# Reordering ScalarE's work around the values of a sparse-attention branch, and copying two pairs of queries on GpSimd

## The chip, the cores and the metric

The kernel runs on one core of a Trainium2 chip. The metric is device time in microseconds (us) for one execution of the whole program, from its inputs in device memory to its output there. A measurement of this kernel is the median of several executions; beside it stands one profiled execution with its trace.

## The reference, cut to what matters

The reference is one layer of a streaming encoder on x of 512 x 1024. A projection feeds two attention branches of 8 heads of 64 each, gates merge the branches, and a gated MLP with a short causal convolution follows. In outline:

```python
proj = x @ w_in
q_a, k_a, v_a, q_i, k_i, w_i, q_s, k_s, v_s, g_a, g_b = split(proj)
# branch A: an indexer scores all keys, 128 of them are kept per query
sel    = top_k(sum_h w_i * relu(q_i . k_i / 8), 128)
p      = softmax(q_a . k_a[sel] / 8 + bias)       # 8 heads
y_a    = p @ v_a[sel]
# branch B: stick-breaking attention, 8 heads
y_s    = stick_break(q_s . k_s / 8) @ v_s
merged = sigmoid(g_a) * (y_a @ w_dsa) + sigmoid(g_b) * (y_s @ w_sb)
x = layer_norm(alpha * x + merged @ w_out)
u, g = split(x @ w_ffn_in)
x = layer_norm(alpha * x + (gelu(conv(u)) * g) @ w_ffn_out)
```

## The kernel before

**Precision.** Every matrix product is done as three matmuls: each operand is split into a high part (type fp32r) and a low part (what is left), and high x high, high x low and low x high are summed in PSUM. So every weight piece of 128 x 1024 that comes from memory is first split. `Stream` does that: its `load` issues the transfer into one of three `raw` buffers (L71), and `_advance` writes the high part with a ScalarE copy (L101, `whi`) and the low part with a subtraction (L107, `wlo`) on VectorE, or on GpSimd for the keys in `POOL_LO`. High and low parts live in rings of three buffers each, so a split needs the buffer of the piece three places before it, and has to wait until TensorE is done with that piece. `st.asp` says by how many pieces the splits run ahead of the piece that is being fetched: 3.

**Order of the work.** `FILL` (L33) lists the projections in the order in which they are used up: ... `qa1 ka1 va bs0 bs1 qa2 ka2 bs2 bs3 qa3 ka3 ga0` .... Here qaN and kaN are the queries and keys of heads 2N and 2N+1 of branch A ("pair N"), va are the values of branch A for all heads, bsN are the gated products of branch B. These pieces are fed as fillers between the steps of the heads. The heads are walked in one list of sixteen: head 0 to 7 are branch B, head 8 to 15 are branch A, so "head 10" is the third head of branch A (`h` = 2 in the code).

**One head of branch A** goes through these steps:

- TensorE makes the logits (`l_ps`, L538), four blocks of queries in three PSUM banks.
- GpSimd has added the bias window and the selection (`bm`, L527) beforehand. VectorE adds `bm` to the logits and takes the minimum (L544), ScalarE takes the exponential (L546). `ups[h]` keeps the exponential traced last.
- `divide` (L549): VectorE divides by the sums (L550, L553). `send_planes` then cuts the result into two 16-bit halves, one copied by ScalarE (L443), one by VectorE (L444), and the sync queue issues two transposing transfers (L446, `pl<-bm`).
- `join_planes` joins the two transposed halves again into `back`, one by ScalarE (L453) and one by VectorE (L454), and then splits the result into high (`pth`, ScalarE, L456) and low (`ptl`, VectorE, L457).
- `weigh` multiplies these with the values (`av_ps`, L471).

In the loop at L660, the turn of head h makes the logits of head h+1, then weighs head h-1, then divides head h+1, then joins head h.

**The values of branch A.** `proj_v("va", ...)` keeps four PSUM banks open, one per block of 128 rows; these are all the banks of the pool `psA`. It takes four weight pieces, va0 to va3. In the last piece the steps are sorted by block, so that the blocks finish one after the other. Then for every block ScalarE copies it out (L261) and VectorE subtracts (L262), which frees the bank. The first matmul that needs a bank of `psA` afterwards belongs to bs0 (L564).

**Doubling the queries.** `stack_dup` puts the 64 rows of one head's queries, high and low part, into one half of a tile of 128 partitions and copies them into the other half: 64 partitions by 1024 elements. That copy is a transfer issued on ScalarE's queue (L337), two for each pair. Its rows are named qa3a, qa3b and so on.

**What sets the order.** The program is traced in Python order. A planner then simulates a timeline and lays down a fixed order for every engine and queue: what its timeline has as ready goes, and what was traced earlier goes first. On the chip each engine runs its list in that order. `tc.issue_after(ins)` adds one rule to it: what is traced inside the block on the engine of `ins` stands behind `ins` on that engine. It says nothing to other engines. At L679 and L681 it is used like this: the division of head 10 stands behind the last value subtraction (VectorE), and VectorE's half of a joining stands behind the division traced just before it.

Of the kernel before, what the change touches and what calls it, by code (L numbers as in the profile page):

```python
# [14 lines left out]
AF = mybir.ActivationFunctionType  # L15
# [33 lines left out]
def r32(ap):  # L49
    return ap.bitcast(F32)  # L50
# [71 lines left out]
def tile_block(ctx: ExitStack, tc: tile.TileContext, xT, xN, w_qi, w_ki, w_t, w_v, w_br, w_o, w_fi, w_fo,  # L122
               bg, cw, rel, onehot, lnp, out):
    nc = tc.nc
# [72 lines left out]
    st = Stream(tc, rawp, ring, order, 3, 3, place, POOL_LO, DMA_LO)  # L197
# [35 lines left out]
    emptied = {}  # L233

    def proj_v(which, name):

        pss = [(pb if which == "vs" else pa)(f"{name}_ps{i}") for i in range(NB)]
        for g in range(4):
            halves = which == "vs" and g == 0
            if not halves:  # L240
                wh, wl = st.get(f"{which}{g}")
            steps = [(kk, i) for kk in range(2) for i in range(NB)]
            if which == "va" and g == 3:
                steps.sort(key=lambda t: t[1])
            for kk, i in steps:
                k = 2 * g + kk
                c = slice(kk * 512, kk * 512 + 512)
                if halves:
                    if i == 0:
                        wh, wl = st.get(f"{which}{g}{kk}")  # L250
                    c = slice(0, 512)
                r = slice(i * 128, i * 128 + 128)
                nc.tensor.matmul(pss[i], xh[k][:, r], wh[:, c], start=(k == 0), stop=False)
                nc.tensor.matmul(pss[i], xh[k][:, r], wl[:, c], start=False, stop=False)
                nc.tensor.matmul(pss[i], xl[k][:, r], wh[:, c], start=False, stop=(k == KC - 1))
                yield 3
        vt = []
        for i in range(NB):
            v = bp.tile([128, H, 2, 64], F32R, tag="v", bufs=4, name=f"{name}{i}")
            src = pss[i].rearrange("p (h d) -> p h d", h=H)  # L260
            nc.scalar.activation(v[:, :, 0, :], src, AF.Copy)  # L261
            emptied[which] = nc.vector.tensor_sub(v[:, :, 1, :], src, r32(v[:, :, 0, :])).ins  # L262
            vt.append(v)
        return vt

# [3 lines left out]
    xh, xl = [], []  # L269
    qps = [pa(f"qi_ps{n}") for n in range(4)]  # L270
    values = proj_v("vs", "vs")
    ohf = bp.tile([64, NREL], F32, tag="beta", bufs=2, name="ohf")
    rbf = padded(bp, [32, H], name="rbf")
# [12 lines left out]
    for k in range(KC):  # L286
        load_x(k + 3)
        xr = xrs.pop(k)
        h = xp.tile([128, 512], F32R, tag="xh", bufs=KC, name=f"xh{k}")
# [40 lines left out]
    def stack_dup(ps, scale, name):  # L330

        a = bp.tile([128, 2, 512], F32R, tag="q", bufs=4, name=f"{name}a")
        b = bp.tile([128, 2, 512], F32R, tag="q", bufs=4, name=f"{name}b")
        for t, own, oth in ((a, slice(0, 64), slice(64, 128)), (b, slice(64, 128), slice(0, 64))):
            nc.scalar.activation(t[own, 0], ps[own], AF.Copy, scale=scale)
            nc.vector.scalar_tensor_tensor(t[own, 1], ps[own], scale, r32(t[own, 0]), op0=ALU.mult, op1=ALU.subtract)
            nc.scalar.dma_start(r32(t[oth]), r32(t[own]))  # L337
        return a, b


# [63 lines left out]
    def select_some(n):  # L404
        for _ in zip(range(n), rounds):
            pass


    def turned():
        return (bp.tile([128, ATT], F32R, tag="th", bufs=1, name="pth"),  # L410
                bp.tile([128, ATT], F32R, tag="tl", bufs=1, name="ptl"))

    def turn_weights(a, off=OFF):

        groups = ((0, ((0, 0),)), (512, ((1, 0), (3, 384))), (1024, ((2, 0),)))
        th, tl = turned()
        parts = []
        for base, grp in groups:
            ps = pb("tr_ps")
            width = 0  # L420
            for i, o in grp:
                for j in range(i, NB):
                    c = off[j] + i * 128
                    nc.tensor.transpose(ps[:, o + (j - i) * 128:o + (j - i) * 128 + 128], a[:, c:c + 128], ident)
                width = max(width, o + 512 - 128 * i)
            w = slice(base, base + width)
            nc.scalar.activation(th[:, w], ps[:, :width], AF.Copy)
            lows = nc.vector.tensor_sub(tl[:, w], ps[:, :width], r32(th[:, w]))
            for i, o in grp:
                c = slice(base + o, base + o + 512 - 128 * i)  # L430
                parts.append((i, slice(128 * i, 512), th[:, c], tl[:, c]))
        parts.sort(key=lambda t: t[0])
        return parts, lows.ins

    def halves16(t):
        return t.bitcast(U16).rearrange("p (c two) -> p two c", two=2)
# [12 lines left out]
    def join_planes(pl):  # L449

        back = bp.tile([128, ATT], F32, tag="back", bufs=1, name="back")
        got = pl.rearrange("p a b c -> p a (b c)")
        nc.scalar.activation(halves16(back)[:, 1], got[:, 1], AF.Copy)  # L453
        nc.vector.tensor_copy(halves16(back)[:, 0], got[:, 0])  # L454
        th, tl = turned()
        nc.scalar.activation(th, back, AF.Copy)  # L456
        nc.vector.tensor_sub(tl, back, r32(th))  # L457
        h, l = (t.rearrange("p (s c) -> p s c", c=128) for t in (th, tl))
        parts = [(i, o, h[:, c], l[:, c]) for i, o, c in
                 ((0, slice(128, 512), slice(0, 9, 3)), (0, slice(0, 128), slice(2, 3)),  # L460
                  (1, slice(128, 512), slice(1, 9, 3)), (2, slice(256, 512), slice(5, 9, 3)),
                  (3, slice(384, 512), slice(9, 10)))]
        return parts
# [42 lines left out]
    def sb_sticks(beta, keep):  # L506

        for j in (0, 2, 3, 1):
            N = 128 * (j + 1)
            lo, hi = OFF[j], OFF[j] + N  # L510
            rev = keep[:, hi:lo:-1]
            scan = nc.vector.tensor_tensor_scan(rev, rev, first[:, 512 - N:512][:, ::-1], 0.0, op0=ALU.mult,  # L512
                                                op1=ALU.max)
        nc.gpsimd.tensor_mul(beta, beta, keep[:, 1:ATT + 1])  # L514
        return scan.ins


    ups = {}
# [83 lines left out]
    def fill(n):  # L602
        while n > 0:
            c = next(fillers, None)
            if c is None:
                return
            n -= c
# [31 lines left out]
    def start_head(i):  # L639
        w, h = heads[i]  # L640
        fill_until(f"q{w}{h//2}", f"k{w}{h//2}")
        if i == H:
            select_some(99)
        args = qk[f"q{w}{h//2}"][h % 2], qk[f"k{w}{h//2}"][h % 2], h
        return sb_head(*args) if w == "s" else dsa_head(*args)

    weights = start_head(0)
    sb_sticks(*weights)
    fill_until("qs1", "ks1")
    def values_of(parts, w, h):  # L650
        if h % 2 == 0:
            pair[w] = bp.tile([128, 512], F32, tag="yt", bufs=2, name=f"y{w}t{h//2}")
        fill_until(f"v{w}")
        ends = weigh(parts, vals[w], h, pair[w])
        if h % 2 == 1:
            (ys if w == "s" else ya).append(finish_pair(pair[w], f"y{w}{h//2}"))
        return ends

    pair, joined = {}, None
    for i, (w, h) in enumerate(heads):  # L660
        following = start_head(i + 1) if i + 1 < len(heads) else ()
        fill(GAP)
        if w == "s":
            parts, lows = turn_weights(weights[0])
            if len(following) == 2:
                with tc.issue_after(lows):
                    scan = sb_sticks(*following)
                with tc.issue_after(scan):
                    select_some(ROUNDS[i])
            fill(GAP)  # L670
            values_of(parts, w, h)
            if len(following) == 1:
                following = following[0]()
        else:
            if joined is not None:
                values_of(*joined)
            fill(GAP)
            if following:
                with tc.issue_after(emptied["va"]) if h == 1 else nullcontext():  # L679
                    following = following[0]()  # L680
                with tc.issue_after(following[1]):  # L681
                    parts = join_planes(weights[0])
            else:
                parts, _ = turn_weights(weights[0], SOFF)
            joined = parts, w, h
        fill(GAP)
        weights = following
# [275 lines left out]
    def bank_c(name):  # L963
        return psC.tile([128, 512], F32, tag="C", bufs=2, name=name)
# [5 lines left out]
    for f in range(2, FC):  # L970
        ups = bank_c("u_ps")
# [240 lines left out]
```

## Time and profile before

| | |
|---|---|
| median of 3 runs | 759.39 us (757.17 to 759.42) |
| the profiled execution | 759.3 us, of which its span is 757.5 us |
| mean granted TensorE clock | 0.996 |
| TensorE (PE) busy | 743.1 us, 98% of the span |
| VectorE (DVE) busy | 564.6 us, 75% |
| ScalarE (ACT) busy | 397.2 us, 52% |
| GpSimd (POOL) busy | 134.2 us, 18% |
| branch A's heads on the timeline | about 188 to 328 us |
| last value matmul of branch A | starts at 225.56 us |

Times of the trace are counted from the start of the span; the 1.8 us by which the execution is longer than its span lie outside of it. The page gives busy times; what sets the end is read from the waits and from the chain that ended last. In a timeline row the columns are the start and the duration in us, the engine, the line of the kernel, the operation, its tiles (written <- read), and in brackets how long the engine stood idle before it and what released it. PEld is TensorE's loading of weights. A name with a small q (SPq, ACTq) is an engine's queue, which issues transfers.

### The profile page before, as it was taken

To read this page: it belongs to the slowest core of one execution; us is meant where nothing else is said; L and a number is where in the kernel's file an instruction comes from. 1 tells how busy PE (TensorE), PEld (TensorE's weight loads), DVE (VectorE), ACT (ScalarE), POOL (GpSimd) and SP (SyncE) were. 2 spreads that over 40 slices of the span, in tenths; PEclk is the share of its full clock that TensorE was granted. 3 is DMA by queue.
4 is the path that set the end of the run, shared out by engine and by line. 5 is a ranking of instruction groups with operands and counts; after the bars stand their busy time and mean duration, and the time that the engine had idled before them with its cause. 6 is when DMAs were issued, how large, how long until landed. Compare 5 with 4: busy or idle time off the path is not lost.

```text
span 757.5 us, 9792 instructions
## 1 busy us (share of the span) xinstructions
PE 743.1 (98%) x3517; PEld 622.3 (82%) x3517; DVE 564.6 (75%) x906; ACT 397.2 (52%) x572; POOL 134.2 (18%) x158
## 2 busy tenths in 40 slices
PE   9999999999999999999999999999999999999996
PEld 7877888888877887888889888888888888888885
DVE  5569777799878795758864867766776767668985
ACT  5475867665575576946364634433443344346430
POOL 0001324223652222000011110011011101110011
PEclk9999999999999999999999999999999999999999
DMA  7445877672374547426823444434444443448542
GB/s 267 149 131 194 206 167 171 137 180 71 98 180 133 146 129 135 119 62 216 333 56 84 139 150 143 158 134 153 139 139 144 148 140 131 147 135 283 195 138 83
DMA packets 60831, 114.80 MB, mean 152 GB/s; under 512 B 29480, under 2 KB 29736, under 8 KB 60784
## 3 DMA queue, kind: packets, MB, share of 16 engines
q1 hardware_dynamic: 53184, 90.70, 38.4%
q0 software_dynamic: 5744, 18.38, 9.7%
q10 hardware_dynamic: 1856, 5.11, 3.0%
q8 instruction: 27, 0.44, 0.3%
q14 instruction: 20, 0.16, 0.1%
HBM read 95.93 MB, written 9.98 MB: 140 GB/s over the span
## 4 chain that ended last, share of the span: by engine, by line
PE 96%; DVE 2%; DMA 1%; ACT 1%; issue 1%; SPq 0%; DVEq 0%; ACTq 0%
PE u_ps L852 5%; PE u_ps L851 5%; PE g_ps L852 5%; PE u_ps L850 5%; PE g_ps L851 5%; PE g_ps L850 5%; PE av_ps L471 3%; PE m L931 2%; PE m L932 2%; PE m L930 2%; PE gb_ps L228 2%; PE ga_ps L229 2%; PE ga_ps L227 2%; PE gb_ps L227 2%; PE gb_ps L229 2%; PE ga_ps L228 2%
## 5 line engine op out<-in xcount | busy, mean ns | idle before, releaser
L101 ACT ACTIVATE whi<-raw 128x1024 fp32r<-128x1024 f32 (+1 forms) x124 | 124.1, 1001 | 172.8 <-PE g_ps L851 45.3
L107 DVE TENSOR_TENSOR wlo<-raw,whi 128x1024 fp32r<-128x1024 f32 (+1 forms) x105 | 123.2, 1174 | 46.7 <-ACT whi L101 46.1
L852 PE MATMUL u_ps<-x1h,wlo 128*128 128x512 f32 (+1 forms) x192 | 71.4, 372 | 0.0
L850 PE MATMUL u_ps<-x1h,whi 128*128 128x512 f32 (+1 forms) x192 | 71.3, 372 | 0.0
L851 PE MATMUL u_ps<-x1l,whi 128*128 128x512 f32 (+1 forms) x192 | 71.3, 371 | 0.0
L850 PE MATMUL g_ps<-x1h,whi 128*128 128x512 f32 (+1 forms) x184 | 69.9, 380 | 0.0
L851 PE MATMUL g_ps<-x1l,whi 128*128 128x512 f32 (+1 forms) x184 | 69.9, 380 | 0.0
L852 PE MATMUL g_ps<-x1h,wlo 128*128 128x512 f32 (+1 forms) x184 | 69.9, 380 | 0.0
L851 PEld LDWEIGHTS u_ps<-x1l,whi 128*128 128x128 f32 x192 | 36.2, 188 | 6.3
L850 PEld LDWEIGHTS u_ps<-x1h,whi 128*128 128x128 f32 x192 | 36.2, 188 | 6.3
L852 PEld LDWEIGHTS u_ps<-x1h,wlo 128*128 128x128 f32 x192 | 36.2, 188 | 6.2
L851 PEld LDWEIGHTS g_ps<-x1l,whi 128*128 128x128 f32 x184 | 34.6, 188 | 6.6
L850 PEld LDWEIGHTS g_ps<-x1h,whi 128*128 128x128 f32 x184 | 34.6, 188 | 6.5
L852 PEld LDWEIGHTS g_ps<-x1h,wlo 128*128 128x128 f32 x184 | 34.6, 188 | 6.5
L527 POOL TENSOR_TENSOR bm<-win,score 128x256 f32<-128x256 f32 (+2 forms) x24 | 29.7, 1265 | 50.4 <-DMA pl<-bm 29.9
L873 DVE TENSOR_TENSOR t<-raw 128x512 f32<-128x512 f32 x11 | 7.6, 692 | 37.8 <-DMA raw<-in_w_fo_dram 37.8
L906 DVE TENSOR_TENSOR hF<-g_ps,c 128x512 f32<-128x512 f32 x22 | 15.1, 687 | 20.8 <-PE g_ps L852 20.8
L898 ACT ACTIVATE c<-c,cwt 128x512 f32<-128x512 f32 x22 | 15.9, 724 | 25.4 <-DVE c L897 25.2
L892 POOL MEMSET u<- 128x2 f32 x22 | 2.1, 99 | 147.1 <-ACT whi L101 101.1
L397 DVE MAX8 m<-score 128x8 f32<-128x256 f32 (+2 forms) x48 | 26.5, 554 | 0.9
L514 POOL TENSOR_TENSOR beta<-beta,keep 128x1280 f32<-128x1280 f32 x8 | 19.6, 2453 | 37.2 <-DVE keep L512 28.3
L748 POOL TENSOR_TENSOR rstd<-rstd,mhalf 128x1 f32<-128x1 f32 x8 | 7.7, 959 | 104.0 <-DVE rstd L747 104.0
(571 smaller groups left out, 2062.4 us busy)
## 6 DMA issues: line engine op xcount, KB each, us to landing
raw<-in_w_fi_dram SPq DMA_DIRECT2D x44, 512.0 KB, 3.3
raw<-in_w_t_dram SPq DMA_DIRECT2D x32, 512.0 KB, 3.4
raw<-in_w_fo_dram SPq DMA_DIRECT2D x26, 512.0 KB, 3.9
wlo<-in_w_t_dram POOLq DMA_DIRECT2D x14, 512.0 KB, 5.5
raw<-in_w_br_dram SPq DMA_DIRECT2D x8, 512.0 KB, 3.3
raw<-in_w_o_dram SPq DMA_DIRECT2D x8, 512.0 KB, 4.0
raw<-in_w_v_dram SPq DMA_DIRECT2D x7, 512.0 KB, 3.3
raw_b<-in_w_fo_dram SPq DMA_DIRECT2D x6, 512.0 KB, 5.5
```

The costliest lines, as they stand in the source:

```text
L101: nc.scalar.activation(hi[:, :w], t[:, :w], AF.Copy)
L107: self.done[key] = eng.tensor_sub(lo[:, :w], t[:, :w], r32(hi[:, :w])).ins
L227: nc.tensor.matmul(ps[:M], wh[:, c], xh[k], start=(k == 0), stop=False)
L228: nc.tensor.matmul(ps[:M], wh[:, c], xl[k], start=False, stop=False)
L229: nc.tensor.matmul(ps[:M], wl[:, c], xh[k], start=False, stop=(k == KC - 1))
L397: nc.vector.max(m8, sc)
L471: nc.tensor.matmul(dst, vt[i][:, h].rearrange("p a d -> p (a d)"), t, start=(n == 0), stop=(n == len(seq) - 1))
L514: nc.gpsimd.tensor_mul(beta, beta, keep[:, 1:ATT + 1])
L527: nc.gpsimd.tensor_add(bm[:, SOFF[j]:SOFF[j] + N], win[:, 512 - N:512], score[j])
L850: nc.tensor.matmul(ps[:, c], wh[:, kc], x1h[:, k, c], start=(k == 0), stop=False)
L851: nc.tensor.matmul(ps[:, c], wh[:, kc], x1l[:, k, c], start=False, stop=False)
L852: nc.tensor.matmul(ps[:, c], wl[:, kc], x1h[:, k, c], start=False, stop=(k == KC - 1))
```

## The change

There are three edits.

1. In `proj_v`, while the piece va3 is fetched, `st.asp` is 2 in place of 3, and 3 again afterwards. The split of qa2, which was traced while va3 was fetched, is now traced with the next fetch (bs0), behind the values' copies and subtractions.
2. `emptied` keeps both the ScalarE copy and the VectorE subtraction of the last value block. What is traced for the division of head 10, and the joining of head 9 that follows it, stands behind both, each on its own engine. Every joining also stands, on ScalarE, behind the last exponential of the next head (`ups[h + 1]`).
3. For qa2 and qa3 the doubling is a GpSimd `tensor_copy` of 64 x 1024 in place of a transfer on ScalarE's queue. The other pairs keep the transfer.

```diff
@@ proj_v
             if not halves:
+                st.asp = 2 if (which, g) == ("va", 3) else 3
                 wh, wl = st.get(f"{which}{g}")
+                st.asp = 3
@@ proj_v, the end
-            nc.scalar.activation(v[:, :, 0, :], src, AF.Copy)
-            emptied[which] = nc.vector.tensor_sub(v[:, :, 1, :], src, r32(v[:, :, 0, :])).ins
+            copied = nc.scalar.activation(v[:, :, 0, :], src, AF.Copy)
+            emptied[which] = copied.ins, nc.vector.tensor_sub(v[:, :, 1, :], src, r32(v[:, :, 0, :])).ins
@@ stack_dup
-            nc.scalar.dma_start(r32(t[oth]), r32(t[own]))
+            if name in ("qa2", "qa3"):
+                nc.gpsimd.tensor_copy(t[oth], r32(t[own]))
+            else:
+                nc.scalar.dma_start(r32(t[oth]), r32(t[own]))
@@ the loop over heads
             if following:
-                with tc.issue_after(emptied["va"]) if h == 1 else nullcontext():
+                behind = emptied["va"] if h == 1 else ()
+                with ExitStack() as ties:
+                    for ins in behind:
+                        ties.enter_context(tc.issue_after(ins))
                     following = following[0]()
-                with tc.issue_after(following[1]):
-                    parts = join_planes(weights[0])
+                    with tc.issue_after(following[1]), tc.issue_after(ups[h + 1]):
+                        parts = join_planes(weights[0])
```

## The prediction

> **What bounds the kernel now.** I read the page first: the busy times, then the chain of work that ended last.
>
> ```profile
> PE 743.1 (98%) x3517; PEld 622.3 (82%) x3517; DVE 564.6 (75%) x906; ACT 397.2 (52%) x572; POOL 134.2 (18%) x158
> ...
> PE 96%; DVE 2%; DMA 1%; ACT 1%; issue 1%; SPq 0%; DVEq 0%; ACTq 0%
> ```
>
> TensorE (PE) is the bound: 98% busy and 96% of the chain. The change takes no matmul away, so it can only win the time in which PE stands or runs slowly. The next view is what PE waits for, over the whole span.
>
> ```profile
> PE bs_ps L564 <- DVE va L262: 3.0, 1, 3.0
> PE l_ps L538 <- issue: 1.5, 1, 1.5
> ```
>
> Two waits lie in branch A, where all three edits lie: 3.0 us at the first product behind the values, and 1.5 us at a head's logits. What else PE waits for comes before branch A. Third, the busy time by stretches (PE, weight loads, DVE, ACT, POOL, then the granted clock, DMA share, GB/s):
>
> ```profile
> 225.00:229.00 4.00, 0.98 (x5) 0.52 (x4) 2.34 (x3) 4.00 (x7) 2.15 (x3) 1.00 0.37 131
> 229.00:233.00 4.00, 4.00 (x13) 3.32 (x13) 3.96 (x10) 0.51 (x2) 0.00 (x0) 0.57 0.65 205
> 299.50:335.00 35.50, 35.50 (x175) 30.14 (x174) 21.85 (x41) 25.32 (x43) 0.00 (x0) 1.00 0.37 107
> ```
>
> For the 4 us behind the first wait the granted clock is 0.57. So that wait costs more than its 3.0 us: 4 x (1 - 0.57) = 1.7 us are lost to the slow clock, and these count as busy. Behind the second, shorter wait the clock stays at 1.00.
>
> **The first wait, place A.** The timeline of ACT, then of DVE and PE, around the end of the values' matmuls (228.81 - 3.02 = 225.8 us, by the PE row):
>
> ```profile
> 223.01 0.73 ACT L546 ACTIVATE lg<-lg,mn 128x512 f32<-128x512 f32 x1 [0.69 <-DVE mn L544]
> 223.64 0.19 ACT L546 ACTIVATION_READ_ACCUMULATOR lg<-lg,mn 128x1 f32 x1
> 224.06 1.68 ACT L453 ACTIVATE back<-pl 128x1280 uint16<-128x1280 uint16 x1 [0.23 <-DMA pl<-bm]
> 225.58 1.05 ACT L101 ACTIVATE whi<-raw 128x1024 fp32r<-128x1024 f32 x1
> 226.51 1.56 ACT L261 ACTIVATE va<-va_ps 128x512 fp32r<-128x512 f32 x3
> 227.95 1.07 ACT L101 ACTIVATE whi<-raw 128x1024 fp32r<-128x1024 f32 x1
> 228.89 0.61 ACT L261 ACTIVATE va<-va_ps 128x512 fp32r<-128x512 f32 x1
> ```
>
> ```profile
> 222.89 1.22 DVE L107 TENSOR_TENSOR wlo<-raw,whi 128x1024 fp32r<-128x1024 f32 x1
> 226.66 1.50 DVE L107 TENSOR_TENSOR wlo<-raw,whi 128x1024 fp32r<-128x1024 f32 x1 [2.55 <-ACT whi L101]
> 228.07 1.87 DVE L262 TENSOR_TENSOR va<-va_ps,va 128x512 fp32r<-128x512 f32 x3
> ```
>
> ```profile
> 228.81 0.50 PE L564 MATMUL bs_ps<-ys0h,whi 128*128 128x512 f32 x1 [3.02 <-DVE va L262]
> ```
>
> PE needs the bank of value block 0, which is free when the first subtraction on line 262 ends (228.07 + 1.87/3 = 228.7). On DVE that subtraction stands behind a weight split (226.66), which waits for its high part on ACT (225.58), which stands behind the joining of head 9 (224.06). Counting the splits back from the four of va on GpSimd, the one at 225.58 is bs1's and the one at 227.95 is qa2's. So the joining is on the path that sets the end, though nobody needs its result yet.
>
> **The second wait, place B.** DVE, ACT, the two queues and PE:
>
> ```profile
> 296.96 1.40 DVE L107 TENSOR_TENSOR wlo<-raw,whi 128x1024 fp32r<-128x1024 f32 x1 [6.18 <-ACT whi L101]
> 298.38 0.69 DVE L544 CUSTOM_DVE_ANT_0 lg<-l_ps,bm 128x512 f32<-128x512 f32 x1
> ```
>
> ```profile
> 282.92 0.47 ACTq L337 DMA_DIRECT2D qa3a<-qa3a  x1
> ...
> 284.79 0.47 ACTq L337 DMA_DIRECT2D qa3b<-qa3b  x1
> ...
> 294.35 1.67 ACT L453 ACTIVATE back<-pl 128x1280 uint16<-128x1280 uint16 x1 [5.71 <-DMA pl<-bm]
> 295.89 1.04 ACT L101 ACTIVATE whi<-raw 128x1024 fp32r<-128x1024 f32 x1
> ```
>
> ```profile
> 272.30 2.91 SPq L446 DMA_TRANSPOSE pl<-bm  x2
> ...
> 282.75 7.36 SPq L446 DMA_TRANSPOSE pl<-bm  x2
> ```
>
> ```profile
> DMA to landing us min/median/max: 3.4/3.5/11.5
> ```
>
> ```profile
> 299.18 0.70 PE L538 MATMUL l_ps<-ka3b,qa3b 128*128 128x512 f32 x2 [1.47 <-issue]
> ```
>
> The transposes of head 13 go out at 282.75, in the same 2 us as the two doublings of pair 3. Their issue takes 7.36 us where the pair before took 2.91, and the slowest transpose lands after 11.5 us where the median is 3.5. ACT waits 5.71 us for it at the joining; the split behind it comes late; DVE stands 6.18 us at that split's low part; behind it stands line 544, which empties the bank of head 14's logits (298.38 + 0.69 = 299.07). PE starts head 15's logits at 299.18. The page names no releaser, but that bank fits to 0.1 us.
>
> **The change part by part.**
>
> *The joining behind the values' copies (place A).* With the joining gone from its place, ACT is free when the exponential's second part ends, at 223.64 + 0.19 = 223.8. Bs1's high part starts there and not at 225.58, and the low part, the first subtraction and PE all move up by the same 1.8 us. PE restarts at about 227.0, after a gap of 1.2 us in place of 3.0. Bounds: 0, if the planner puts something else as long there; 3.0, if it puts block 0's copy and subtraction ahead of bs1's split, since three quarters of the last piece's matmuls come behind block 0's. I take 1.8: bs1's split is traced earlier than the copies.
>
> *The slow clock behind it.* A gap of 1.47 us left the clock at 1.00, a gap of 3.02 brought 0.57. A gap of 1.2 lies on the side of the former: 1.7 us won. Bounds 0 and 1.7. [...]
>
> *The split of qa2 behind the copies.* It takes 1.07 us of ACT from between the third and fourth value copy, and a low part of 1.2 us (the row at 222.89) from DVE. That brings block 3 and head 10's division forward; PE has other products by then, so 0. If qa2's own split comes later, the cover is the products of bs0 and bs1, which come before qa2's; without it the 1.07 + 1.2 = 2.3 us of the split would be seen there.
>
> *Joinings behind the next head's exponentials.* Same instructions, later on ACT. The farthest move is head 11's, from ahead of head 12's logits to behind its exponentials. There the profile has
>
> ```profile
> 270.05 1.06 ACT L101 ACTIVATE whi<-raw 128x1024 fp32r<-128x1024 f32 x1 [1.77 <-PE bs_ps L565]
> ```
>
> ```profile
> 270.14 0.91 DVE L454 COPY back<-pl 128x1280 uint16<-128x1280 uint16 x1
> ```
>
> an ACT that stands 1.77 us where the joining needs 1.68, ahead of VectorE's half at 270.14, which sets the end of the joining already. So 0. At place B the joining no longer holds up ACT while its transpose is under way: this alone removes the wait there.
>
> *GpSimd's copies for pairs 2 and 3.* Removed: four transfers, 4 x 0.47 us of ACT's queue. Added: four copies of 64 x 1024 on GpSimd. The nearest rows:
>
> ```profile
> L619 POOL CAST oh<-ohf x1: 714/714/714, 19.0 to 19.0; 64x640 fp32r<-64x640 f32 x1
> ```
>
> ```profile
> L107 POOL TENSOR_TENSOR wlo<-raw,whi 128x1024 fp32r<-128x1024 f32 x5 | 12.5, 2499 | 2.7 <-ACT whi L101 2.7
> ```
>
> From below 0.71 x 1024/640 = 1.1 us, from above 2.5 us, which has two inputs; I take 1.3, nearer to the row of its own kind. GpSimd is 18% busy. The copies end some 2 to 4 us after their inputs, the transfer of qa3b took 9.3 us to land. With them gone the transposes have the DMA engines to themselves: at place B a second cure of the same wait. Won there, by either: 1.5 us, bounds 0 and 1.5.
>
> The sum: 1.8 + 1.7 + 1.5 = 5.0 us. The profiled execution took 759.3 us, 0.1 below the median of the runs, and 759.3 - 5.0 = 754.3.
>
> **The rivals.**
>
> *Half of it.* The gap at A stays long enough for the slow clock, or B stays. For it speaks that nothing here shows the clock between gaps of 1.47 and 3.02, and that the planner's order isn't seen. 759.3 - 1.8 - 1.5 = 756.0, or 759.3 - 1.8 - 1.7 = 755.8.
>
> *The wait moves to the next pair's queries.* PE is 3.5 us earlier behind A, but if VectorE isn't, the logits of heads 12 and 14 wait for their queries and keys:
>
> ```profile
> 260.74 0.69 DVE L327 TENSOR_TENSOR ka2b<-ka_ps,ka2b 64x512 fp32r<-64x512 f32 x1
> ```
>
> ```profile
> 264.00 1.43 PE L538 MATMUL l_ps<-ka2a,qa2a 128*128 128x512 f32 x8
> ```
>
> ```profile
> 279.95 2.34 DVE L107 TENSOR_TENSOR wlo<-raw,whi 128x1024 fp32r<-128x1024 f32 x1
> ```
>
> Slack there is 264.0 - 261.4 = 2.6 us, so 3.5 - 2.6 = 0.9 comes back. And a split on DVE took 2.34 us in place of 1.22 with GpSimd's additions just before and beside it; if each new copy stretches DVE like that, 1.1 us, the four give back 4.5. Together 5.4 of 5.0: 759.7, no change. Against it: the division of head 10 is earlier too, so VectorE's work moves with PE, and it stood 6.2 us ahead of B. [...]
>
> *Slower: a doubling queued behind head 15's additions on GpSimd.* One queue, in order:
>
> ```profile
> 295.56 3.92 POOL L527 TENSOR_TENSOR bm<-win,score 128x256 f32<-128x256 f32 x3 [14.26 <-DMA pl<-bm]
> ```
>
> These additions wait for the transposes of head 13. If the planner sets qa3a's copy behind them, and they land as late as before, the additions end 3.5 us earlier than in that row at 296.0, the copy at 297.3, and head 14's logits, due at 292.6 - 3.5 = 289.1, wait 8 us, with 1.7 us of slow clock behind it: 754.3 + 9.7 = 764. It decides as soon as the transposes land later than some 285; without the collision of place B they should land about then, which speaks against it.
>
> **How the numbers follow.** Forecast 0.60, half 0.15, no change 0.14, slower 0.11. The time predicted is 754.3. Its own range is 753.0 (all of A: 3.0 + 1.7 + 1.5 = 6.2 won, rounded) to 755.0. The range for 8 in 10 runs from 752.8 to 758.4: the half case and the better end of the one without change. What a measurement of this kernel can tell from no change is about 0.3%, 2.3 us: faster 0.75, same 0.14, slower 0.11.
>
> **What would show it.** Right: the wait of bs_ps for va is 1.5 us or less, and the clock is at 1.00 in the 4 us behind it; on ACT the copies of line 261 stand ahead of the joining of head 9; no issue on line 337 for qa2 and qa3, four GpSimd copies of 1.1 to 2.5 us; head 13's transposes issue in about 2.9 us; the wait of 1.5 us at l_ps is gone; PE's busy time is 1 to 2 us less, since slow matmuls count as busy. Wrong: a new wait of over 1 us at l_ps or av_ps between 229 and 300 us, a clock below 1 there, or an order on DVE that puts more than one split ahead of the first value subtraction.

## The result, and the profile after

The changed kernel takes **754.56 us** (median of 5 runs, 754.16 to 755.98), the kernel before 759.05 us (median of 5, 757.17 to 759.42). The ratio is 0.9948 with a 95% interval of 0.9932 to 0.9965: 4.5 us won by the medians, where 754.3 us was predicted. The profiled execution took 754.56 us with a span of 752.8 us, against 759.3 and 757.5 before: 4.7 us.

Its page, the busy times and the chain that ended last:

```profile
PE 741.5 (99%) x3517; PEld 621.2 (83%) x3517; DVE 567.4 (75%) x906; ACT 397.3 (53%) x572; POOL 137.7 (18%) x162
...
PE 88%; DVE 7%; ACT 2%; issue 1%; DMA 1%; POOL 0%; SPq 0%; DVEq 0%; ACTq 0%; POOLq 0%
```

TensorE is busy for 1.6 us less with the same 3517 matmuls, so part of the gain is matmuls that run faster, and the rest is standing that went. What TensorE waits for, over the whole span:

```profile
PE idle_ps L204 <- DVE idle L201: 1.2, 1, 1.2
PE dot_ps L385 <- ACT relu L388: 1.0, 1, 1.0
PE bs_ps L569 <- DVE va L264: 0.9, 1, 0.9
PE vs_ps L255 <- ACT whi L101: 0.5, 1, 0.5
```

The wait at place A (bs_ps for va) is 0.9 us where it was 3.0, and the wait at a head's logits, place B, is not in the list any more. The stretches around place A (columns as in the prediction: PE, weight loads, DVE, ACT, POOL, then the granted clock):

```profile
225.00:229.00 4.00, 3.12 (x16) 2.36 (x15) 3.76 (x7) 4.00 (x7) 3.63 (x4) 1.00 0.73 234
229.00:233.00 4.00, 4.00 (x22) 3.38 (x21) 4.00 (x8) 1.88 (x2) 0.00 (x0) 1.00 0.42 135
```

The 4 us in which the clock was at 0.57 now have 1.00, and 22 matmuls begin in them in place of 13. How place A came about, on the timeline of ScalarE, then VectorE, then TensorE:

```profile
224.13 1.04 ACT L101 ACTIVATE whi<-raw 128x1024 fp32r<-128x1024 f32 x1
225.08 2.03 ACT L263 ACTIVATE va<-va_ps 128x512 fp32r<-128x512 f32 x4
226.99 1.08 ACT L101 ACTIVATE whi<-raw 128x1024 fp32r<-128x1024 f32 x1
227.94 1.67 ACT L458 ACTIVATE back<-pl 128x1280 uint16<-128x1280 uint16 x1
```

```profile
225.21 1.22 DVE L107 TENSOR_TENSOR wlo<-raw,whi 128x1024 fp32r<-128x1024 f32 x1 [0.70 <-ACT whi L101]
226.35 2.47 DVE L264 TENSOR_TENSOR va<-va_ps,va 128x512 fp32r<-128x512 f32 x4
```

```profile
227.09 0.50 PE L569 MATMUL bs_ps<-ys0h,whi 128*128 128x512 f32 x1 [0.88 <-DVE va L264]
```

On ScalarE the order is now bs1's high part, the four value copies, qa2's high part, and only then the joining of head 9. On VectorE the four value subtractions stand together behind bs1's low part.

Place B, in the order GpSimd, sync queue, ScalarE, VectorE:

```profile
279.45 1.50 POOL L340 CAST qa3a<-qa3a 64x1024 fp32r<-64x1024 f32 x1 [3.26 <-DVE qa3a L338]
281.01 1.04 POOL L340 CAST qa3b<-qa3b 64x1024 fp32r<-64x1024 f32 x1
```

```profile
279.20 4.30 SPq L451 DMA_TRANSPOSE pl<-bm  x2
```

```profile
293.26 1.65 ACT L458 ACTIVATE back<-pl 128x1280 uint16<-128x1280 uint16 x1
```

```profile
290.32 0.69 DVE L549 CUSTOM_DVE_ANT_0 lg<-l_ps,bm 128x512 f32<-128x512 f32 x1
```

Both things that the change did there can be seen. The transposes of head 13 issue in 4.30 us in place of 7.36, and the joining that needs them stands on ScalarE behind the exponentials of head 14 and waits for nothing. The first bank of head 14's logits is emptied at 290.32 us where it was 298.38: 8 us earlier, more than all that the kernel gained.

**The gain by places.** The gap at A is 3.02 - 0.88 = 2.1 us shorter, the slow clock behind it was worth 1.7 us, the wait at B 1.5 us: 5.3 us. From it goes what the timeline lost before it came to place A. The values' matmuls of the kernel before and of the changed one (the numbers on both sides of "to" are the starts of the first and of the last matmul):

```profile
L255 PE MATMUL va_ps<-whi,xl x32: 388/389/397, 200.4 to 225.4; 128*128 128x512 f32 x32
```

```profile
L257 PE MATMUL va_ps<-whi,xl x32: 388/389/398, 200.8 to 225.8; 128*128 128x512 f32 x32
```

That is 0.4 us later, in work that the change doesn't touch (0.2 of it in the wait of vs_ps, 0.3 us before and 0.5 us here). 5.3 - 0.4 = 4.9, of 4.7 us measured between the two profiled executions. The last 0.2 us were not followed. This is an account of these two executions; what the other runs say of its terms comes with the experiments.

### The profile page after: what moved, and what is told of

Its sections match the earlier page's. It is cut to its first block, busy times and chain, and to the rows that moved or that the text cites. A ratio compares the mean times of both kernels' runs of the same rounds, so it can differ in the third digit from the quotient of the medians.

```text
span 752.8 us, 9797 instructions
## 1 busy us (share of the span) xinstructions
PE 741.5 (99%) x3517; PEld 621.2 (83%) x3517; DVE 567.4 (75%) x906; ACT 397.3 (53%) x572; POOL 137.7 (18%) x162
## 4 chain that ended last, share of the span: by engine, by line
PE 88%; DVE 7%; ACT 2%; issue 1%; DMA 1%; POOL 0%; SPq 0%; DVEq 0%; ACTq 0%; POOLq 0%
PE u_ps L860 5%; PE u_ps L859 5%; PE g_ps L860 5%; PE u_ps L858 5%; PE g_ps L859 5%; PE g_ps L858 5%; PE m L939 2%; PE m L940 2%; PE m L938 2%; PE av_ps L476 2%; PE ga_ps L228 2%; PE ga_ps L227 2%; PE ga_ps L229 2%; PE o_ps L789 2%; PE o_ps L787 2%; PE o_ps L788 2%
## 5 line engine op out<-in xcount | busy, mean ns | idle before, releaser
L532 POOL TENSOR_TENSOR bm<-win,score 128x256 f32<-128x256 f32 (+2 forms) x24 | 27.6, 1178 | 33.3 <-DMA pl<-bm 25.9
```

The source lines that it names most:

```text
L532: nc.gpsimd.tensor_add(bm[:, SOFF[j]:SOFF[j] + N], win[:, 512 - N:512], score[j])
```

## The experiments

Two questions were open. Which of the three edits brings the gain, and does each act where the prediction put it? And is the slow clock behind place A a price of the gap itself, or of what else happens there? Ratios are to the kernel before, run on the same chip in the same batch.

### One edit at a time: ties_only, copies_only, ahead_only

`ties_only` is the kernel before with edit 2 alone (the division of head 10 and the joinings tied behind the values' copies and the exponentials):

```diff
+            copied = nc.scalar.activation(v[:, :, 0, :], src, AF.Copy)
+            emptied[which] = copied.ins, nc.vector.tensor_sub(v[:, :, 1, :], src, r32(v[:, :, 0, :])).ins
...
+                    for ins in behind:
+                        ties.enter_context(tc.issue_after(ins))
                     following = following[0]()
+                    with tc.issue_after(following[1]), tc.issue_after(ups[h + 1]):
+                        parts = join_planes(weights[0])
```

> Edit 2 alone: the joinings and head 10's division behind the values' copies and behind the next head's exponentials on ScalarE; qa2's split and the doublings as before. The theory (the joining of head 9 on ScalarE is what PE waits for at place A, and the joining of head 13 at place B): the wait of bs_ps is 0.9 to 1.3 us in place of 3.0, the clock behind it 1.00, the wait at l_ps is gone although the transposes of head 13 still take over 7 us to issue; 754.3 to 755.0 us, nearly the whole gain. Rival (qa2's split ahead of the last value copy is what costs at A): the wait of bs_ps is 2 us or more, 757. Rival (the collision of the doublings with the transposes is what costs at B): the wait of 1.5 us at l_ps stays, 756.

Measured: 755.44 us (754.4 to 757.98, 12 runs), ratio 0.996 [0.9943, 0.9977].

`copies_only` is the kernel before with edit 3 alone:

```diff
+            if name in ("qa2", "qa3"):
+                nc.gpsimd.tensor_copy(t[oth], r32(t[own]))
+            else:
+                nc.scalar.dma_start(r32(t[oth]), r32(t[own]))
```

> Edit 3 alone: GpSimd copies the doubled queries of pairs 2 and 3. The theory (two independent cures at place B): A as before, 3.0 us of wait and a clock near 0.57 behind it; at B the transposes of head 13 issue in 3 to 4.5 us, the joining no longer stands, the wait of 1.5 us at l_ps is gone: 757.5 us. Rival (only the order on ScalarE cures B): the wait at l_ps stays, 759.0. Rival (the copies stretch VectorE's work): over 759.5.

Measured: 758.04 us (755.93 to 759.61, 12 runs), ratio 0.9991 [0.9974, 1.0008].

`ahead_only` is the kernel before with edit 1 alone:

```diff
+                st.asp = 2 if (which, g) == ("va", 3) else 3
                 wh, wl = st.get(f"{which}{g}")
+                st.asp = 3
```

> Edit 1 alone: qa2's split is traced behind the values' copies. The theory (it adds nothing for PE): the joining of head 9 and bs1's split keep their places ahead of the value copies, so the wait of bs_ps is 3.0 us with a clock near 0.57 and the wait of 1.5 us at l_ps stays: 759.0 us, no change. Rival (qa2's split is what holds the values' copies): the wait of bs_ps falls below 1.5 us, 755.5.

Measured: 759.64 us (756.22 to 765.02, 12 runs), ratio 1.0017 [0.999, 1.0044].

Edit 2 alone is the only one that is measurably faster. Place A by the waits and by the 4 us behind it, in ties_only and then in copies_only:

```profile
PE bs_ps L564 <- DVE va L262: 1.8, 1, 1.8
```

```profile
229.00:233.00 4.00, 4.00 (x20) 3.39 (x19) 3.96 (x10) 1.31 (x2) 0.00 (x0) 1.00 0.50 169
```

```profile
PE bs_ps L567 <- DVE va L262: 3.0, 1, 3.0
```

```profile
229.00:233.00 4.00, 3.78 (x10) 3.22 (x11) 3.96 (x9) 0.93 (x2) 0.00 (x0) 0.50 0.58 166
233.00:237.00 4.00, 4.00 (x15) 3.36 (x14) 2.24 (x5) 1.27 (x1) 0.00 (x0) 0.70 0.51 149
```

With the joining out of the way the gap falls to 1.8 us and the clock stays at 1.00. With the copies alone the gap is what it was, and the slow clock with it. In ahead_only the gap is 2.9 us and the clock 0.57: moving qa2's split does nothing while the joining still stands ahead of bs1's split.

At place B, neither ties_only nor copies_only has a wait at l_ps any more, and ahead_only keeps one of 1.0 us. The transposes of head 13 in ties_only and in copies_only:

```profile
279.66 6.84 SPq L446 DMA_TRANSPOSE pl<-bm  x2
...
DMA to landing us min/median/max: 3.4/5.2/9.6
```

```profile
282.95 4.08 SPq L449 DMA_TRANSPOSE pl<-bm  x2
...
DMA to landing us min/median/max: 3.4/3.9/4.9
```

In ties_only they are as slow as ever (9.6 us to the last landing), but nobody stands at them: the joining comes behind head 14's exponentials, at 293.5 us. In copies_only the joining still stands in its old place, at 288.2 us, but they land after 4.9 us and ScalarE does not stand there. So in these traces they are two separate cures of one wait.

What the wait is worth in time is less clear than the trace's 1.5 us. The mean granted clock of a run tells how long it ran slowly, so runs with the same mean clock can be compared. At 0.993 the median of copies_only is 759.6 us and that of the kernel before 760.0, at 0.995 it is 758.0 against 758.6, at 0.997 (two and five runs) 756.3 against 756.0. That is half a microsecond or nothing, so a gain of 1.5 us at place B is not shown by the times.

### Without the copies: no_copies

Edits 1 and 2, without edit 3:

```diff
-            if name in ("qa2", "qa3"):
-                nc.gpsimd.tensor_copy(t[oth], r32(t[own]))
-            else:
-                nc.scalar.dma_start(r32(t[oth]), r32(t[own]))
+            nc.scalar.dma_start(r32(t[oth]), r32(t[own]))
```

> Edits 1 and 2 without edit 3. The theory: equal to the changed kernel, 754.3 to 755.2 us; the transposes of head 13 take over 7 us to issue beside the two doublings, but behind the exponentials nobody waits for them. Rival (the copies carry the gain at place B): the wait of 1.5 us at l_ps is back, 756.0.

Measured: 754.91 us (753.86 to 756.93, 10 runs), ratio 0.9945 [0.9924, 0.9966]. That is the changed kernel's ratio, so the GpSimd copies add nothing measurable to the other two edits. The transposes issue in 7.88 us here and the last lands after 11.8, the slowest of all these kernels, and TensorE has no wait at l_ps. At place A there is one difference to the changed kernel. VectorE and GpSimd:

```profile
224.62 2.10 DVE L107 TENSOR_TENSOR wlo<-raw,whi 128x1024 fp32r<-128x1024 f32 x1 [0.69 <-ACT whi L101]
```

```profile
223.91 3.94 POOL L529 TENSOR_TENSOR bm<-win,score 128x256 f32<-128x256 f32 x3 [3.09 <-DMA pl<-bm]
```

Bs1's low part takes 2.10 us beside GpSimd's additions, and the gap is 1.8 us, as in ties_only (2.09 us). In the changed kernel the same low part took 1.22 us and the gap was 0.9. It was 0.9 in a second traced execution of the changed kernel too (`changed_again`, below), so this isn't chance of one run. But the additions run beside the low part there as well, from 224.52 us for 4.03 us:

```profile
224.52 4.03 POOL L532 TENSOR_TENSOR bm<-win,score 128x256 f32<-128x256 f32 x3 [3.11 <-DVE wlo L107]
```

Between the two kernels the starts differ. In the changed kernel the low part starts at 225.21 us, just before GpSimd's second addition (128 x 384) at 225.22, and takes 1.22 us; the addition takes 2.06, where in the kernel before, with no subtraction beside it, it took 1.01. In no_copies the additions start at 223.91 us. If the second follows 0.70 us behind the first, as it does in the changed kernel, it starts at about 224.61 us (an estimate), just before the low part at 224.62. The low part takes 2.10 us there, and the three additions together take 3.94, where they took 2.94 in the kernel before. Ties_only and values_tie_only go like no_copies (low parts of 2.09 and 2.06 us, additions of 3.94 and 3.93), changed_again like the changed kernel (1.23 and 4.03). So in all five traces the additions took 1.0 to 1.1 us more than in the kernel before, and in the three where the low part by that estimate started second it took 0.8 to 0.9 us more than 1.22 as well. Why was not tested.

### Halves of edit 2: values_tie_only, ups_tie_only

`values_tie_only` ties the division of head 10 and the joining of head 9 behind the values' copies, without the rule on the exponentials:

```diff
+                behind = emptied["va"] if h == 1 else ()
+                with ExitStack() as ties:
+                    for ins in behind:
+                        ties.enter_context(tc.issue_after(ins))
                     following = following[0]()
+                    with tc.issue_after(following[1]):
+                        parts = join_planes(weights[0])
```

> Half of edit 2 alone: head 10's division and head 9's joining behind the values' copies on ScalarE; the other joinings, qa2's split and the doublings as before. The theory (place A and place B have nothing to do with each other): the wait of bs_ps is 0.9 to 1.8 us and the clock behind it 1.00; the transposes of head 13 still run beside the doublings, the joining stands for them on ScalarE, and a wait of 1 to 1.5 us at l_ps stays: 756.0 us. Rival (place B came from being late behind place A): no wait at l_ps, 754.8.

Measured: 755.85 us (754.37 to 762.05, 10 runs), ratio 0.9965 [0.9943, 0.9987]; gap at A 1.8 us, clock 1.00 behind it.

`ups_tie_only` has only the rule on the exponentials:

```diff
-                with tc.issue_after(following[1]):
+                with tc.issue_after(following[1]), tc.issue_after(ups[h + 1]):
                     parts = join_planes(weights[0])
```

> The other half of edit 2 alone: every joining behind the next head's exponentials on ScalarE, not behind the values' copies. The theory: place A as before (3.0 us of wait, slow clock), since head 10's exponentials stand ahead of head 9's joining anyway; place B cured although the transposes of head 13 are as slow as before (7 us to issue): no wait at l_ps, 757.6 us. Rival (the exponentials' tie also frees the values' copies): the wait of bs_ps is under 2 us, 755.

Measured: 757.98 us (756.01 to 760.54, 10 runs), ratio 0.9985 [0.9965, 1.0004]; gap at A 3.0 us, clock 0.50 in 229 to 233 us.

So by the traces the half that acts at place A carries the gain. At place B both brought a surprise. In values_tie_only, where neither cure is in, the transposes and the joining were:

```profile
280.21 6.51 SPq L446 DMA_TRANSPOSE pl<-bm  x2
...
DMA to landing us min/median/max: 6.1/7.5/8.9
```

```profile
289.15 1.67 ACT L453 ACTIVATE back<-pl 128x1280 uint16<-128x1280 uint16 x1 [3.05 <-DMA pl<-bm]
```

ScalarE does stand at the joining, 3.05 us in place of 5.71, and TensorE shows no wait at l_ps: the stall is there but just short enough to be covered. I had expected 1 to 1.5 us to remain, and that is wrong for this execution; the rival of the expectation, no wait at l_ps, is what it shows. Some runs of it are longer than the clock explains (757.33 and 757.87 us at a mean granted clock of 0.997, where others have 754.4). They have no trace, so whether the wait comes back in those is open.

In ups_tie_only the joining is out of the way and TensorE waits all the same:

```profile
PE l_ps L538 <- DMA qa3a<-qa3a: 1.2, 1, 1.2
```

```profile
284.12 5.92 SPq L446 DMA_TRANSPOSE pl<-bm  x2
```

Here the doubling is issued at 284.3 us, beside these transposes, and takes 11.3 us to land, where it took 5.5 in the kernel before, so that head 14's logits wait for their own queries. This is a second way in which the collision can cost time, which the prediction did not have. With edit 3 there is no such transfer: the changed kernel's trace has GpSimd's copies of 1.50 and 1.04 us in its place, and no wait at l_ps.

### The clock by itself: bs1_high_x2, bs1_high_x3

Both are the changed kernel, made slower at place A alone, by writing bs1's high part more than once (the same values, two times in the first, three times in the second):

```diff
-            nc.scalar.activation(hi[:, :w], t[:, :w], AF.Copy)
+            for _ in range(2 if key == "bs1" else 1):
+                nc.scalar.activation(hi[:, :w], t[:, :w], AF.Copy)
```

In bs1_high_x3 the value subtractions are also tied behind bs1's low part on VectorE.

> The changed kernel with bs1's high part written twice on ScalarE (the same values again, one more pass of about 1.0 us ahead of the first value copy): only the length of the gap at the first product behind the values is changed. Theory that the slow clock is a price of the gap's length with an edge between 1.8 and 2.9 us: the gap goes from 0.9 to 1.8-1.9 us (to 2.7 if bs1's low part takes 2.1 us again as it did in three looks), the granted clock in the 4 us behind it stays at 1.00 for a gap up to 1.9, and the time is 754.6 + 0.9 = 755.5 us. Rival, a loss in proportion to the gap: the clock behind a gap of 1.9 falls to some 0.75 for 4 us, and the time is 756.5 us.

> The changed kernel with bs1's high part written three times on ScalarE and the value subtractions of va behind bs1's low part on VectorE: the gap at the first product behind the values is made as long as it was before the change, or a little longer (0.9 + 2 x 0.95 = 2.8 us, 3.3 to 3.6 with a low part of 2.1), while joinings, division and GpSimd's copies stay as the change has them. Theory (the gap itself brings the slow clock, whatever stands around it): clock 0.5 to 0.6 in the 4 us behind it, time 754.6 + 2.0 to 2.6 + 1.7 or more = 758.3 to 759.2 us, and no wait at head 14's or 15's logits. Rival (the slow clock came from what else was under way at that moment, such as the joining of head 9 on ScalarE and its transposes): the clock stays at 1.00 and the time is 756.6 to 757.2 us.

Measured, against 758.15 us of the kernel before in this batch: bs1_high_x2 758.99 us (756.21 to 759.78, 10 runs), ratio 0.9997 [0.9974, 1.0019]; bs1_high_x3 760.06 us (757.24 to 760.47, 10 runs), ratio 1.002 [1.0005, 1.0036]. The gaps became 3.0 and 3.5 us. In bs1_high_x2 it is 2.1 more than in the changed kernel and not 1.0 more, because the low part took 2.21 us again. So the first of the two did not test a gap of 1.9 us, as was meant. The second came out above the 758.3 to 759.2 us that were expected. But both show that the gain is lost when the gap alone comes back, with every joining, division and copy where the change has them: all of it by the medians, while the interval of bs1_high_x2 would leave up to 2 us of the 4.5. The slow clock does not need the joining of head 9 ahead of the copies. The stretches of bs1_high_x2, 1 us each, and then of the kernel before:

```profile
228.00:229.00 1.00, 0.00 (x0) 0.00 (x0) 1.00 (x2) 1.00 (x2) 0.00 (x0) 0.75 0.00 0
229.00:230.00 1.00, 0.78 (x2) 0.69 (x3) 1.00 (x3) 1.00 (x2) 0.00 (x0) 0.50 0.31 86
...
234.00:235.00 1.00, 1.00 (x4) 0.81 (x3) 0.30 (x1) 0.84 (x1) 0.00 (x0) 0.50 0.82 270
235.00:236.00 1.00, 1.00 (x5) 0.81 (x5) 0.33 (x1) 0.00 (x0) 0.00 (x0) 0.83 0.50 201
```

```profile
228.00:229.00 1.00, 0.19 (x1) 0.19 (x2) 1.00 (x3) 1.00 (x3) 0.00 (x0) 1.00 0.00 0
229.00:230.00 1.00, 1.00 (x4) 0.75 (x4) 1.00 (x3) 0.51 (x2) 0.00 (x0) 0.64 0.77 205
230.00:231.00 1.00, 1.00 (x6) 1.00 (x5) 1.00 (x1) 0.00 (x0) 0.00 (x0) 0.50 0.82 320
231.00:232.00 1.00, 1.00 (x4) 0.81 (x4) 0.96 (x4) 0.00 (x0) 0.00 (x0) 0.50 0.06 16
232.00:233.00 1.00, 1.00 (x4) 0.76 (x4) 1.00 (x5) 0.00 (x0) 0.00 (x0) 0.65 0.94 279
```

In these slices the clock is at 1.00, at 0.50, or changes between the two. In the kernel before it is at 0.50 for (0.36 + 0.50 + 0.50 + 0.35) / 0.50 = 3.4 us, in bs1_high_x2, where all stretches from 229 to 235 have 0.50, for (0.25 + 6 x 0.50 + 0.17) / 0.50 = 6.8 us. Worked out in the same way, ahead_only has 3.4 us, and copies_only, ups_tie_only and bs1_high_x3 have 6.8. No trace showed another length at place A. So in these six traces the price of the slow clock comes in steps: half of 3.4 us is 1.7, half of 6.8 is 3.4 (some 0.3 less in these four traces, where the first 0.6 to 0.7 us of it fall into the gap itself).

For the runs without a trace there is only the mean granted clock. Bs1_high_x2 has two at 0.997 (756.2 and 756.3 us), two at 0.995 (757.4 and 757.6) and six at 0.993 or 0.994 (758.9 to 759.8). One step is 1.7 us of 757, or 0.002 of the mean clock, so these fit to none, one and two steps. The kernel before shows the same spread: in this batch 7 of its 19 runs are at 0.997 or above, and the others go down to 0.992. Of the changed kernel's 13 runs, 12 are at 0.997 or 0.998. Not every run fits: two of the kernel before took 761.56 and 761.97 us at 0.994.

All six traces with a gap of 2.9 us or more show the slow clock; none of the five with one of 0.9 or 1.8 us does, nor does the one without a gap. What makes it last 3.4 or 6.8 us, and why by the mean clocks the same kernel pays none, one or two of these steps, no run shows. In ups_tie_only the last value matmul ends at 226.1 us and this slice shows where the clock falls:

```profile
228.00:229.00 1.00, 0.00 (x0) 0.00 (x0) 1.00 (x3) 1.00 (x2) 0.00 (x0) 0.68 0.00 0
```

A mean of 0.68 means that the clock fell 0.36 us into it, at 228.4 us. TensorE had stood for 2.3 us by then, and what came later can't have brought it about. Whether 1.8 us can be enough is open: no trace shows it, but four of the 32 runs of ties_only, no_copies and values_tie_only are at 0.995 or below.

### Going on: bs1_last, and the changed kernel again

What is left at place A is bs1's own split, which also isn't needed yet. `bs1_last` puts it behind the last value copy on ScalarE and behind the last value subtraction on VectorE:

```diff
-                st.asp = 2 if (which, g) == ("va", 3) else 3
+                st.asp = {("va", 2): 2, ("va", 3): 1}.get((which, g), 3)
...
+        if which == "va":
+            st.behind["bs1"] = emptied[which]
...
+            with ExitStack() as ties:
+                for ins in self.behind.get(key, ()):
+                    ties.enter_context(self.tc.issue_after(ins))
+                nc.scalar.activation(hi[:, :w], t[:, :w], AF.Copy)
...
```

> The changed kernel, and bs1's split as well stands behind the last value copy (ScalarE) and the last value subtraction (VectorE). The theory (what is left at place A is bs1's split ahead of the first value subtraction): the wait of bs_ps for the values is 0.3 us or less; bs1's low part is ready some 229 us, its matmuls start about 233 us; no new wait: 0.9 us less than the changed kernel, 753.7 us. Rival (bs1 comes late for its own matmuls): a wait of bs_ps for wlo of over 0.5 us, 754.6 or more.

> The changed kernel once more, beside the run before: 754.6 us. Its wait of bs_ps was 0.9 us; by the runs without the copies it depends on how long VectorE takes for bs1's low part beside GpSimd's additions (1.2 or 2.1 us), so 0.9 to 1.8 us here, and the clock behind it 1.00.

Measured: bs1_last **753.59 us** (752.85 to 753.7, 5 runs), ratio 0.9927 [0.9909, 0.9944]; the changed kernel beside it 755.4 us (754.23 to 757.91, 8 runs), ratio 0.9949 [0.9929, 0.9969]. The slowest run of bs1_last is faster than every run of the changed kernel. The two profiled executions, 753.59 and 754.23 us, are 0.6 us apart. Its ScalarE, VectorE and TensorE at place A:

```profile
224.24 1.55 ACT L269 ACTIVATE va<-va_ps 128x512 fp32r<-128x512 f32 x3
226.33 0.60 ACT L269 ACTIVATE va<-va_ps 128x512 fp32r<-128x512 f32 x1 [0.55 <-PE va_ps L263]
226.83 2.00 ACT L104 ACTIVATE whi<-raw 128x1024 fp32r<-128x1024 f32 x2
```

```profile
224.85 1.89 DVE L270 TENSOR_TENSOR va<-va_ps,va 128x512 fp32r<-128x512 f32 x3 [0.23 <-ACT va L269]
```

```profile
226.13 0.39 PE L577 MATMUL bs_ps<-ys0h,whi 128*128 128x512 f32 x1
```

The first value subtraction ends at 224.85 + 1.89/3 = 225.5 us, while TensorE is still at the last value blocks, and the first product starts without a gap. In its list of TensorE's waits none is left in branch A.

## Why the prediction came out

**The sum** was 1.8 + 1.7 + 1.5 = 5.0 us, of 4.7 measured between the profiles and 4.5 between the medians. Between the two traces the gain lies at the two places named, and the signs that were named are there: the wait at bs_ps is below 1.5 us with a clock of 1.00 behind it, the wait at l_ps is gone, PE is busy for 1.6 us less.

**The joining behind the values' copies: 1.8 taken, 2.1 measured.** Against the last value matmul, bs1's high part starts 0.2 us later in the kernel before (225.58 against 225.4) and 1.7 us earlier in the changed one (224.13 against 225.8): 1.9 us of movement, which is the step as it was worked out. What was not foreseen is the low part behind it. I carried over its 1.50 us; it took 1.22 here, and 2.1 in ties_only, no_copies and values_tie_only. So the gap of 1.2 us that was forecast never occurred: it was 0.9 or 1.8 us, and by the estimate of the starts a low part some hundredths of a us ahead of GpSimd's second addition, or behind it, went with the one or the other. Nothing in the prediction told which.

**The slow clock: 1.7 taken, 1.7 measured, and still half right.** That a gap of about 1 us keeps the clock at 1.00 held, and a loss in proportion to the gap, 1.2/3.0 x 1.7 = 0.7 us, with which the range goes up to 754.3 + 0.7 = 755.0, is a term that no run shows: behind the traced gaps of 0.9 and 1.8 us the 4 us have a clock of 1.00. But I took 1.7 us as what a gap of 3.0 us costs. It is what it cost in one execution; two other traces with that gap (copies_only and ups_tie_only) show 3.1 us, and by their mean clocks some runs pay nothing. That one step was in the profiled execution, and that this execution lay near the median, was luck: with another execution the same working would have given a sum up to 1.7 us larger or smaller.

**Place B: 1.5 taken, 1.5 measured between the two traces.** That either edit 2 or edit 3 removes the wait is shown by ties_only and copies_only, each with its own mechanism as the prediction had it. In the times it is not seen: copies_only can't be told from the kernel before, and at the same mean clock it is 0.6 us faster at best. Two things were missing. The collision can also hold up head 14's own queries (ups_tie_only, 1.2 us), which joinings in another place don't help. And the wait is marginal: when place A was cured alone it also vanished, in the one execution that was traced.

**The split of qa2: 0 taken, 0 measured** (ahead_only, 1.0017 [0.999, 1.0044]). **Joinings elsewhere: 0 taken**, and the list of waits shows no new one at av_ps or l_ps.

**GpSimd's copies: 1.3 us each taken.** Pair 3's took 1.50 and 1.04 us; pair 2's both took 1.04:

```profile
252.93 1.04 POOL L340 CAST qa2a<-qa2a 64x1024 fp32r<-64x1024 f32 x1
254.03 1.04 POOL L340 CAST qa2b<-qa2b 64x1024 fp32r<-64x1024 f32 x1
```

The estimate from the smaller copy, 1.1 us, was the better one here; in other kernels single copies took up to 2.19 us (copies_only). One sign was wrong: the transposes of head 13 were to issue in 2.9 us and took 4.30. With the doublings gone something else still lengthens it, and what it is was not followed; since the joining no longer waits, it costs nothing. So the prediction's sentence that the transposes would then have the DMA engines to themselves is not borne out here. The longest issue of a single one is 2.79 us here; in bs1_last none takes over 2.32.

**The rivals.** No wait moved to the next pair's queries, and no copy ended up behind head 15's additions: qa3b's copy runs at 281.01 us, 8 us before head 14's first logits are emptied and ahead of those additions, which start at 285.80 us. "Half of it" occurred as a mechanism in single-edit kernels, not in the change. That VectorE's work can be longer beside GpSimd's, from which the 4.5 us of the rival with no change came, was seen at place A: low parts of 2.06 to 2.10 us beside the additions in three traces, and the other way round the addition of 2.06 us beside the low part of 1.22. The copies had a price too. Of VectorE's subtractions, a low part that started at 254.26 us, behind the start of qa2b's copy, took 1.89 us in place of 1.22, and the one of line 462 at 281.28, behind the start of qa3b's, 2.12 in place of the 1.49 of the same head's in the kernel before. That is 1.3 us where the rival had 4.5, and TensorE's list of waits shows none that came of it.

**Who did the work.** Edit 2 alone brings 0.996 and edits 1 and 2 together 0.9945, all three 0.9948: within the intervals these are one number. The copies' own gain (0.9991) and that of qa2's split (1.0017) can't be told from nothing.

## What to carry to other kernels

When the bounding engine stands, follow the chain behind the releaser through each engine's fixed order, and look for work in it that nobody needs yet: here it was a joining, and then, one step on, a weight split. A gap on TensorE of 2.9 to 3.5 us cost 1.7 us (two traces) or 3.1 us (four traces) more than itself here, in steps that by the mean clocks differ from run to run, so one profile can show too little or too much of what removing it wins. The times were steadier without it: the 5 runs of bs1_last lie within 0.9 us, the 10 of bs1_high_x2 within 3.6. Behind gaps of 0.9 and 1.8 us no trace shows such a price; taking the last 0.9 us away won 0.6 us between the two profiled executions. And where two edits each remove the same wait, try each alone before counting both.

## What the runs showed of the hardware that was not expected

- The slow clock comes in lengths of 3.4 or 6.8 us at exactly 0.50, in six traces with gaps of 2.9 to 3.5 us. By the mean clocks its number of steps goes with the spread of the runs of bs1_high_x2. In other kernels there are runs that it doesn't explain, such as 757.98 us of ties_only at 0.998. Bs1_last, which has no gap there, spreads over 0.9 us, bs1_high_x2 over 3.6 us.
- The same subtraction of 128 x 1024 on VectorE took 1.22, 1.50, 2.1 or 2.2 us at place A. It took 1.22 us with GpSimd idle (bs1_high_x3), 1.50 where it started at 226.66 us, 0.41 us before the end of GpSimd's last addition (the kernel before), and 2.21 where GpSimd was busy for 1.57 of the 2 us from 226 to 228 (bs1_high_x2). In no_copies it took 2.10 us, with the three additions at 3.94 us in place of 2.94. In the changed kernel it started 0.01 us ahead of the addition of 128 x 384 and took 1.22 us, and that addition 2.06 in place of 1.01.
- Two doublings of 64 x 1024 issued on ScalarE's queue in the same microseconds as two transposes go with a later landing: the transposes' last landing was at 5.0 us at most in four traces without the doublings there (the changed kernel, changed_again, copies_only, bs1_last) and at 8.9 to 11.8 in six with them. The first doubling's own landing took 4.8 to 5.9 us in four of these six (the kernel before, ties_only, no_copies, values_tie_only) and 11.3 in ups_tie_only.
